# One decoder layer on one core: where the gate_r blocks, the squares of x and the embedding products stand, and how wide the attention products of the later keys are

## The chip, the cores and the metric

The kernel runs on one core of a Trainium2 chip. Its time is the device time of one execution, in microseconds (us). A core has TensorE (matrix products, which accumulate into PSUM), VectorE and ScalarE (elementwise work; ScalarE also evaluates functions and loads a table when the function's set changes), GpSimd, and SyncE, whose queue (SP) issues the DMAs. In the profile they are PE (with PEld for the loads of the stationary operand), ACT for ScalarE, DVE for VectorE, POOL for GpSimd, SP for SyncE. PSUM has eight banks of 128 x 512 floats here.

## The reference

One layer of a decoder for 256 tokens of width 2048, in float32.

```
h = rmsnorm(x, g_mix)
x_r, g_r, q, k, v, gate_r, gate_a = split(h @ w_in)       # 2816, 2816, then 5 of 2048
xc  = causal depthwise conv of width 4 (x_r)
r, i = sigmoid(block-diagonal products of xc + biases)     # 16 blocks of 176
a   = exp(-8 r softplus(-lambda));  u = sqrt(1 - a^2) * i * xc
s_t = a_t s_(t-1) + u_t                                    # scan over the tokens
y_r = (gelu(g_r) * s) @ w_rnn_out
q, k = rmsnorm per head (16 heads of 128)
z = q k^T / sqrt(128), only keys before the query
w = exp(log_sigmoid(z) + sum over later keys of log_sigmoid(-z))
y_a = (w @ v) @ w_attn_out
x = x + (sigmoid(gate_r) * y_r + sigmoid(gate_a) * y_a) @ w_o
x = x + (silu(g) * u) @ w_ffn_down,   g, u = split(rmsnorm(x, g_ffn) @ w_ffn_gu)   # 5632 each
x = x + sigmoid(rmsnorm(x, g_ple) @ w_ple_gate) * (p @ w_ple_proj)
```

## The kernel before

**Precision.** Every float32 operand is cut into a high part, rounded to the type that TensorE takes in one pass (`F32R`), and a low part, the rest. A product is three matmuls: high by high, high by low, low by high. `prod` (L534 to 538) does this with the activations as the stationary operand and 512 columns of weights moving, so its output is tokens x features; `mm3` (L447) the same for other operands; `dense` (L456) has a weight tile stationary and x moving, once with 512 columns (high and low part of x side by side, L466) and once with 256 (L470), so its output is features x tokens.

**Weights.** All weights lie packed in DRAM in the order in which they are used. `plan()` writes that order: one entry per block of products, cut into chunks of at most eight 128 x 128 tiles (512 KB; the first entry begins with two chunks of four tiles, `cuts_of`). `Stream` loads the chunks on the SP queue (`dma_to`, four buffers `w32`), up to 4 chunks ahead, and splits them up to 3 chunks ahead: ScalarE makes the high part (`whi`, L272), VectorE the low part (`wlo`, L273), four buffers each. `S_.after` hangs the load of another pair of rows of x (256 KB) behind a chunk. `Block` gives the split tiles of one entry to the code that uses them.

**Order of work.** The program is written in one order, and a planner in the build (the tile framework with its timeline) orders each engine's instructions by that order and by when it reckons that their operands are ready, and gives out buffers and PSUM banks. The engines then run their lists strictly in order.

**Stages.**

1. x comes transposed, 128 features x 256 tokens per row, in eight tiles `xt` of two rows. `next_xg` multiplies a tile by the gain and splits it (`xg`). `norm_sq` adds the squares of a tile to `acc0` (ScalarE squares, VectorE adds); `norm_end` sums over the partitions on TensorE (L519) and makes `rstd`, the scale of each token, along the free dimension; `norm_tokens` (L600) makes the same scales along the partitions, `rstd_tok`, with matmuls of two columns (L606).
2. The first product is a `dense` of four tiles: x_r for recurrence pairs 0 and 1 (L710). In its middle `norm_x` does all eight squares.
3. The recurrence, 11 pairs of 128 features (`for p in range(NPR)`, L714): `rnn_g` (projection g_r and gelu), for p up to 8 the projection and convolution of x_r for pair p + 2 (`rnn_conv`), and `rnn_gates` (the block-diagonal products, then sigmoid, exp, tanh, sqrt, the scan, and a split of the result). Behind pairs 1, 4, 6 and 9 (`GATE_R_AT`, L81) stands a gate_r block: `gate` and `block` (L689), 16 rows x 2 token halves x 3 matmuls of 512 columns, then a sigmoid.
4. The tail (`tail()`, L148) is a list of groups. `group` (L727) makes a 256 x 1024 output: both token halves by two column blocks, in four banks named 2, 4, 3, 8. Part of its rows go through a Strassen-like scheme with seven products in place of eight ("11", "T1", ... in the lists `SEVEN`, `SEVEN3`, `LONG`); it needs sums of weight tiles on VectorE (`Stream.summed`) and a fifth bank, B. `whole` (L775) joins the banks with the scheme's partial results. `pend` is a list of small tasks (transposes and splits for a later stage), one of which is done per weight row of a group.
5. Attention is laid over the q, k and gate_a blocks, two heads at a time (`step`, `ATT_AT`). Queries are 256 columns, keys two tiles of 128. `att_z` (L857) makes z with `mm3`, `att_e` the weights, `att_o` (L907) the products with v. For the second key tile (keys 128 to 255) the first 128 queries have no part: `att_z` computes them all the same, and `att_o` reads tiles `w1h`, `w1l`, in which those columns hold zeros (L391).
6. The last two groups (`pg`, L1071 on): `whole` gives the gate product, a sigmoid with the token scale, then for each column block and token half the embedding product (`p` by `w_ple_proj`, 6 matmuls), a multiplication, the addition of x1, and the store of 128 x 512 outputs (L1084). In the plan the two embedding chunks ("x", 0) and ("x", 1) stand at the end of the group.

Of the kernel before, what the change touches and what calls it, by code (L numbers as in the profile page):

```python
# [36 lines left out]
TWO = (0, 1)  # L37
NEG = -1e30
# [42 lines left out]
GATE_R_AT = {1: 0, 4: 1, 6: 2, 9: 3}  # L81


def plan():
# [6 lines left out]
    def proj(c0, p):  # L91
        dense("in", c0 + 2 * p, range(KD))
# [17 lines left out]
    dense("in", C_XR, range(KD), nt=4)  # L110
    for p in range(NPR):
        proj(C_GR, p)
        if p + 2 < NPR:
            proj(C_XR, p + 2)
        gates(p)
        if p in GATE_R_AT:
            block(C_GTR, GATE_R_AT[p])

    def tokens(name, g, w, cols, slots):


        for x in slots:
            if isinstance(x, int):
                t = [(w, x, m) for c in cols for m in c]
            elif x[0] == "x":
                t = [("pp", k, m) for k in range(2) for m in cols[x[1]]]
            elif isinstance(x, tuple):
                p = 2 * x[2]
                t = {1: [(p, 0), (p + 1, 0)], 2: [(p + 1, 1), (p, 1)]}.get(x[1], [])
                t = [(w, k, m) for k, c in t for m in cols[c]]  # L130
            elif x in ("T2", "T3", "T4"):
                t = []
            else:
                r, c = {"11": (0, 0), "21": (1, 0), "22": (1, 1), "T1": (0, 1)}[x]
                t = [(w, 2 * p + r, m) for p in TWO for m in cols[c]]
            out.append((("tok", name, g, x), t))

# [10 lines left out]
def tail():  # L148
# [11 lines left out]
    def dn(q):  # L160
# [8 lines left out]
            + wide("pg", "pg", [SEVEN + x] * 2))  # L169


TAIL = tail()
# [120 lines left out]
class Block:  # L293
# [7 lines left out]

    def chunk(self, c):
        a = self.cuts[c - 1] if c else 0
        return [(x, self[x]) for x in range(a, self.cuts[c])]
# [9 lines left out]
def tile_hybrid_block(ctx: ExitStack, tc: tile.TileContext, xT: bass.AP, x: bass.AP, pT: bass.AP,  # L314
# [53 lines left out]
    S_.dma_to(1)  # L368
    nc.sync.dma_start(t0[:, 256:], xT[:, 1, :])
    S_.after = {i: next_x for i in range(1, NPD)}  # L370
    S_.dma_to(2)
    nc.sync.dma_start(prm_sb, prm)
    S_.dma_to(4)
# [215 lines left out]
    for i in range(3):  # L589
        next_xg()  # L590
        S_.split_to(i + 2)

    def norm_x():
        with tc.issue_after(S_.hi_ins.ins):
            for i in range(NPD):
                norm_sq(xt[i], acc0, i == 0)

    rstd_tok = cst.tile([P, 4], F32, tag="rstdt", name="rstd_tok")

    def norm_tokens(acc, r):  # L600

        pn = psum()
        for t in range(2):
            for e in range(2):
                c = e * 256 + t * P
                nc.tensor.matmul(pn[:, 2 * t:2 * t + 2], acc[:, c:c + P], ones[:, :2],  # L606
                                 start=(e == 0), stop=(e == 1))
        rsqrt_mean(r, pn[:, :4], D)
# [92 lines left out]
    def rs_x(t):  # L701
        return rstd_tok[:, 2 * t:2 * t + 1]
# [7 lines left out]
    p01 = dense(in_keys(C_XR, 0), xg, 4, norm_x, next_xg)  # L710
    norm_end(acc0, rstd)
    rnn_conv(0, sums(p01[:2]))
    rnn_conv(1, sums(p01[2:]))
    for p in range(NPR):  # L714
# [3 lines left out]
        if p == 0:  # L718
            with tc.issue_after(S_.lo_ins.ins):
                decay_scales()  # L720
            norm_tokens(acc0, rstd_tok)
# [5 lines left out]
    def group(at, pairs, sums, after=None, also=()):  # L727

        name, g = at
        slots = [x for n, y, _, _, _, sl in TAIL if (n, y) == at for x in sl
                 if isinstance(x, int) or is_sum(x)]
        seq = [(n, q) for n, x in enumerate(slots) for q in products(x)]
        first, last = {}, {}
        for i, (_, (b, y, _, _)) in enumerate(seq):
            first.setdefault(b, i)  # L740
            last[b] = i
            if y in ("11", "T1", "T2", "T3"):
                last[y] = i
        plain8 = [i for i, (_, (b, y, _, _)) in enumerate(seq) if b == "8" and not isinstance(y, str)]
        assert "11" not in last or last["T1"] < plain8[0]
        banks, tile_ = {}, {}
        for i, (n, (b, y, p, c)) in enumerate(seq):
            if i == 0 or seq[i - 1][0] != n:
                if n in also:
                    also[n]()  # L750
                if n >= 3 and pend:
                    pend.pop(0)()
                w_ = S_.take(("tok", name, g, slots[n]))[0]
            if b not in banks:
                banks[b] = psum()
            ps = banks[b]
            if p is None:
                o = tok(pairs, *y)
            else:
                o = {"11": tok(pairs, 2 * p, 0), "21": tok(pairs, 2 * p + 1, 0), "22": sums[p][3],  # L760
                     "T1": sums[p][0], "T2": sums[p][1], "T3": sums[p][2],
                     "T4": tok(pairs, 2 * p + 1, 1)}[y]
            s = slice(c * 512, c * 512 + 512)
            prod(ps, o, w_[2][:, s], w_[3][:, s], i == first[b], i in (last[b], last.get(y)),
                 b in "B8")
            if y in ("11", "T1", "T2", "T3") and i == last[y]:
                t = tile_[y] = tl("T")
                actv(t, ps, AF.Copy)
                if y == "T2":
                    tt(tile_["T1"], tile_["T1"], t, ALU.subtract)  # L770
                if y == "T3" and after is not None:
                    after(tile_)
        return [banks[b] for b in "2438"], tile_

    def whole(at, pairs, sums, also=()):  # L775

        (q2, q4, q3, q8), t = group(at, pairs, sums, None, also)
        c11, c21, c12, c22 = t["11"], t["T3"], t["T1"], t["T2"]
        tt(c11, q2, c11, ALU.add)
        tt(c12, q3, c12, ALU.add)  # L780
        tt(c22, q8, c21, ALU.subtract)
        tt(c21, q4, c21, ALU.add)
# [74 lines left out]
    def att_z(hp):  # L857
        qt, kt_ = qs.pop(hp), ks.pop(hp)
        pss = []
        for kt in range(2):  # L860
            ps = psum()
            for e in range(2):
# [3 lines left out]
                mm3(o, (k_[:, c:c + P], k_[:, 256 + c:256 + c + P]), q_[:, :256], q_[:, 256:],  # L866
                    True, True)
# [39 lines left out]
    def att_o(hp):  # L907
        ws = zst.pop(hp)
        ps = psum()
        for e in range(2):  # L910
            o = ps[:, e * 256:e * 256 + 256]
            s = slice(e * 256, e * 256 + 256)
            for kt in range(2):
                v_ = vs[hp // 4 * 4 + hp // 2 % 2 * 2 + kt]
                c = hp % 2 * 256 + e * P
                mm3(o, (v_[:, c:c + P], v_[:, 512 + c:512 + c + P]), ws[kt][0][:, s],
# [153 lines left out]

    for g in range(2):  # L1071
        gate_ = whole(("pg", g), h3, sum3)
        for n, c in enumerate(gate_):
            actv(c, c, AF.Sigmoid, scale=rs2[:, n % 2:n % 2 + 1])
        for b in range(2):
            w_ = S_.take(("tok", "pg", g, ("x", b)))[0]
            for t in range(2):
                ps, c, x_ = psum(), gate_[2 * b + t], x1[t][2 * g + b]
                for k in range(2):
                    s = slice(k * 512, k * 512 + 512)  # L1080
                    prod(ps, tok(pts, k, t), w_[2][:, s], w_[3][:, s], k == 0, k == 1)
                tt(c, ps, c, ALU.mult)
                tt(c, c, x_, ALU.add)
                nc.sync.dma_start(out[t * P:t * P + P, (2 * g + b) * 512:(2 * g + b) * 512 + 512], c)  # L1084
# [62 lines left out]
```

## Time and profile before

| | |
|---|---|
| median of 3 runs | 1896.11 us (1894.04 to 1896.20) |
| the profiled execution | 1897.69 us, of which span 1896.0 us |
| mean granted TensorE clock | 0.998 |
| TensorE busy | 1881.1 us, 9006 matmuls |
| VectorE busy | 1379.6 us, 1646 instructions |
| ScalarE busy | 1160.1 us, 1532 instructions |
| read from HBM | 357.69 MB, 190 GB/s over the span |

The span runs from the first to the last instruction. Matmuls overlap: one of 512 columns is recorded with 391 ns, but the next starts some 227 ns after it, so the pace is read from the starts. A line such as `PE L466 MATMUL ps<-Q,whi 128x512 f32 x8` names engine, line of the kernel, output and inputs, the shape of the moving operand, and how many are merged; its first two numbers are start and length in us. What stands in brackets is the time that the engine was idle before it, and who ended that.

### The profile page before, as it was taken

How to read it: one execution, taken by the hardware profiler on the slowest of the kernel's cores; microseconds unless marked ns; L12 is line 12 of the kernel's file. 1: busy time of each engine (PE TensorE's matmuls, PEld its weight loads, DVE VectorE, ACT ScalarE, POOL GpSimd, SP SyncE). 2: the span in 40 equal slices, each digit the busy share in tenths (PEclk: the TensorE clock that was granted, in tenths of full speed). 3: DMA queues.
4: the chain of work that ended last, by engine and by line, in shares of the span. 5: the costliest groups of instructions: out<-in, count | busy, mean ns of one | idle time of the engine just before them, and what ended most of it. 6: DMA issues, size and time to landing. Idle time of an engine off the chain costs nothing.

```text
span 1896.0 us, 24012 instructions
## 1 busy us (share of the span) xinstructions
PE 1881.1 (99%) x9006; PEld 1581.3 (83%) x9006; DVE 1379.6 (73%) x1646; ACT 1160.1 (61%) x1532; POOL 2.2 (0%) x9
## 2 busy tenths in 40 slices
PE   8999999999999999999999999999999999999998
PEld 7988888888888888888888888888888888888887
DVE  7877676776687566665478988866886688855776
ACT  6878787874455566667445776644664456544663
POOL 0000000000000000000000000000000000000000
PEclk9999999999999999999999999999999999999999
DMA  6555555465635544545565555476356635565454
GB/s 239 176 197 178 204 175 194 168 227 191 247 134 193 194 157 156 178 152 171 194 228 200 205 190 215 173 251 218 134 186 242 235 123 208 180 211 191 166 193 150
DMA packets 101781, 361.36 MB, mean 191 GB/s; under 512 B 11424, under 2 KB 11808, under 8 KB 101664
## 3 DMA queue, kind: packets, MB, share of 16 engines
q1 hardware_dynamic: 101520, 359.82, 54.7%
q8 instruction: 70, 1.15, 0.2%
q14 instruction: 47, 0.39, 0.1%
q10 hardware_dynamic: 144, 0.01, 0.0%
HBM read 357.69 MB, written 2.10 MB: 190 GB/s over the span
## 4 chain that ended last, share of the span: by engine, by line
PE 93%; ACT 3%; DVE 2%; issue 1%; DMA 1%; SPq 0%; DVEq 0%; ACTq 0%
PE ps L537 26%; PE ps L538 26%; PE ps L536 26%; PE ps L466 7%; PE ps L470 4%; ACT H L347 1%; ACT L347 1%; PE ps L448 1%; PE ps L449 1%; PE ps L450 1%; DVE H L341 1%; DVE wlo L273 1%; ACT whi L272 1%; PE ps L1043 1%; DMA w<-in_w_dram 0%
## 5 line engine op out<-in xcount | busy, mean ns | idle before, releaser
L273 DVE TENSOR_TENSOR wlo<-w,whi 128x1024 fp32r<-128x1024 f32 (+3 forms) x580 | 701.1, 1215 | 361.3 <-ACT whi L272 357.4
L272 ACT ACTIVATE whi<-w 128x1024 fp32r<-128x1024 f32 (+3 forms) x580 | 606.3, 1052 | 465.6 <-PE ps L538 394.7
L537 PE MATMUL ps<-wlo,Q 128*128 128x512 f32 x2223 | 869.9, 391 | 3.1 <-DVE wlo L273 3.1
L538 PE MATMUL ps<-whi,Q 128*128 128x512 f32 x2223 | 868.1, 391 | 0.0
L536 PE MATMUL ps<-whi,Q 128*128 128x512 f32 x2223 | 796.5, 392 | 1.6 <-ACT whi L272 1.3
L537 PEld LDWEIGHTS ps<-wlo,Q 128*128 128x128 f32 x2223 | 418.4, 188 | 90.7 <-DVE wlo L273 6.0
L538 PEld LDWEIGHTS ps<-whi,Q 128*128 128x128 f32 x2223 | 418.4, 188 | 85.9
L536 PEld LDWEIGHTS ps<-whi,Q 128*128 128x128 f32 x2223 | 417.0, 188 | 87.4 <-ACT whi L272 2.0
L272 ACT ACTIVATE whi<-Q 128x1024 fp32r<-128x1024 f32 (+1 forms) x177 | 182.8, 1033 | 135.9 <-PE ps L538 117.5
L273 DVE TENSOR_TENSOR wlo<-Q,whi 128x1024 fp32r<-128x1024 f32 (+1 forms) x177 | 210.4, 1190 | 53.5 <-ACT whi L272 53.3
L466 PE MATMUL ps<-Q,whi 128*128 128x512 f32 x704 | 172.9, 395 | 1.1 <-ACT whi L272 1.1
L466 PEld LDWEIGHTS ps<-Q,whi 128*128 128x128 f32 x704 | 130.5, 191 | 26.6 <-ACT whi L272 1.9
L341 DVE TENSOR_TENSOR H<-ps,H 128x512 f32<-128x512 f32 (+1 forms) x168 | 99.0, 616 | 30.4 <-ACT H L347 16.2
L470 PEld LDWEIGHTS ps<-Q,wlo 128*128 128x128 f32 x704 | 91.1, 193 | 6.5 <-DVE wlo L273 2.9
L470 PE MATMUL ps<-Q,wlo 128*128 128x256 f32 x704 | 92.6, 284 | 2.5 <-DVE wlo L273 2.5
L256 DVE TENSOR_TENSOR Q<-Q,Q 128x1024 f32<-128x1024 f32 x76 | 92.8, 1221 | 0.8
L347 ACT ACTIVATE H<-ps 128x512 f32<-128x512 f32 (+1 forms) x122 | 60.2, 514 | 50.9 <-PE ps L466 31.1
L347 ACT ACT_TABLE_LOAD x66 | 84.7, 1283 | 2.7 <-DVE cT L574 1.5
L341 DVE TENSOR_TENSOR H<-H,H 128x512 f32<-128x512 f32 (+1 forms) x106 | 63.3, 604 | 1.8 <-ACT H L347 1.3
L347 ACT ACTIVATE Q<-H 128x512 fp32r<-128x512 f32 x41 | 25.2, 626 | 26.2 <-DVE H L341 25.7
L347 ACT ACTIVATE Q<-ps 128x512 fp32r<-128x512 f32 (+2 forms) x52 | 27.8, 565 | 19.7 <-DVE ps L341 8.8
L448 PE MATMUL ps<-Q,whi 128*128 128x256 f32 x140 | 39.7, 284 | 0.0
(131 smaller groups left out, 870.6 us busy)
## 6 DMA issues: line engine op xcount, KB each, us to landing
w<-in_w_dram SPq DMA_DIRECT2D x558, 512.0 KB, 3.8
Q<-in_w_dram SPq DMA_DIRECT2D x98, 512.0 KB, 6.7
w<-in_w_dram SPq DMA_DIRECT2D x16, 448.0 KB, 3.2
H<-in_x_dram SPq DMA_DIRECT2D x8, 256.0 KB, 5.9
out_dram<-H SPq DMA_DIRECT2D x8, 256.0 KB, 3.0
H<-in_xT_dram SPq DMA_DIRECT2D x7, 256.0 KB, 7.6
w<-in_w_dram SPq DMA_DIRECT2D x4, 320.0 KB, 5.1
w<-in_w_dram SPq DMA_DIRECT2D x2, 256.0 KB, 3.4
```

The costliest lines, as they stand in the source:

```text
L256: self.nc.vector.tensor_tensor(r[o], r[o], r[a], ALU.add)
L272: self.hi_ins = self.nc.scalar.activation(hi[:, :c], t[:, :c], AF.Copy)
L273: self.lo_ins = self.nc.vector.tensor_tensor(lo[:, :c], t[:, :c], hi[:, :c].bitcast(F32), ALU.subtract)
L341: nc.vector.tensor_tensor(o, a, b, op)
L347: nc.scalar.activation(o, i, f, **kw)
L448: nc.tensor.matmul(o, wt[0], xh, start=start, stop=False)
L449: nc.tensor.matmul(o, wt[0], xl, start=False, stop=False)
L466: nc.tensor.matmul(pss[e], wt[0], rhs(xs, k), start=(k == 0), stop=(k == n - 1))
L470: nc.tensor.matmul(pss[e][:, :256], wt[1], rhs(xs, k)[:, :256], start=False, stop=False)
L536: nc.tensor.matmul(ps, x[0], wh, start=start, stop=False, skip_group_check=goes_on)
L537: nc.tensor.matmul(ps, x[0], wl, start=False, stop=False, skip_group_check=goes_on)
L538: nc.tensor.matmul(ps, x[1], wh, start=False, stop=stop, skip_group_check=goes_on)
```

## The change

1. A new first group `("gtr", 0)` (list `HEAD`) computes gate_r blocks 0 and 1, all 16 rows of x plain, with `group`, which moves up in the file. The x_r products for pairs 0 and 1 follow as two ordinary projections. The other two gate_r blocks stand behind pairs 5 and 10.
2. In that group, the rows of x are scaled one tile per two chunks, and the squares of one tile are taken per chunk (slots 4 to 11). `x_scales` (slot 13) makes `rstd` as before and gets `rstd_tok` from it by two transposes; `norm_tokens` goes. A load of x hangs behind every second chunk; the second half of the first x tile and the parameters are loaded later in the queue.
3. The embedding chunks stand ahead of the last three rows of both last groups, and `embedded` makes their four products there. In the very last group (`LAST_GROUP`) the last three rows are not done row by row but bank by bank: all of 2, then 4, 3, 8. Each bank then gets its own run of join, sigmoid, multiplication, addition and store; the very last in two halves of 256 columns.
4. In `att_z` and `att_o` the matmuls of the second key tile have 128 query columns in place of 256.
5. `whole` joins in the order of the banks, with other tiles for two of the results.

```diff
-GATE_R_AT = {1: 0, 4: 1, 6: 2, 9: 3}
+GATE_R_AT = {5: 2, 10: 3}
...
-    dense("in", C_XR, range(KD), nt=4)
...
+    for stage, g, w, c0, c1, slots in HEAD:
+        tokens(stage, g, w, [list(range(c, c + 4)) for c in (c0, c1)], slots)
+    proj(C_XR, 0)
+    proj(C_XR, 1)
...
-            + wide("pg", "pg", [SEVEN + x] * 2))
+            + wide("pg", "pg", [SEVEN[:-3] + x + SEVEN[-3:]] * 2))
+HEAD = [("gtr", 0, "in", C_GTR, C_GTR + 4, list(range(KD)))]
...
     S_.dma_to(1)
+    S_.after = {2 * i: next_x for i in range(1, NPD)}
+    S_.dma_to(2)
     nc.sync.dma_start(t0[:, 256:], xT[:, 1, :])
-    S_.after = {i: next_x for i in range(1, NPD)}
-    S_.dma_to(2)
+    S_.dma_to(4)
     nc.sync.dma_start(prm_sb, prm)
-    S_.dma_to(4)
...
-    for i in range(3):
+    for i in range(2):
         next_xg()
         S_.split_to(i + 2)
...
+    def x_scales():
+        norm_end(acc0, rstd)
+        ps = psum()
         for t in range(2):
...
+            nc.tensor.transpose(ps[:, t * P:t * P + P], rstd[:, t * P:t * P + P], ident)
+            actv(rstd_tok[:, t:t + 1], ps[:, t * P:t * P + 1], AF.Copy)
...
+        if at == LAST_GROUP:
+            k = len(slots) - 3
+            rest = [q for q in seq if q[0] >= k]
+            seq = [q for q in seq if q[0] < k] + [q for b in "2438" for q in rest if q[1][0] == b]
...
-    p01 = dense(in_keys(C_XR, 0), xg, 4, norm_x, next_xg)
-    norm_end(acc0, rstd)
-    rnn_conv(0, sums(p01[:2]))
-    rnn_conv(1, sums(p01[2:]))
...
+    for i in range(2, NPD):
+        also.setdefault(2 * i - 3, []).append(next_xg)
+    for i in range(NPD):
+        also.setdefault(4 + i, []).append((lambda i: lambda: norm_sq(xt[i], acc0, i == 0))(i))
+    also[13] = [x_scales]
...
+    pss = group(("gtr", 0), xg, None, None, also)[0]
+    for b in range(2):
+        gtr.append([tl("C") for _ in range(2)])
+        for t in range(2):
+            actv(gtr[b][t], pss[2 * b + t], AF.Sigmoid, scale=rs_x(t))
+    for p in range(2):
+        rnn_conv(p, from_x(C_XR, p, "T", scale=False))
...
-                mm3(o, (k_[:, c:c + P], k_[:, 256 + c:256 + c + P]), q_[:, :256], q_[:, 256:],
-                    True, True)
+                mm3(o[:, c:], (k_[:, c:c + P], k_[:, 256 + c:256 + c + P]), q_[:, c:256],
+                    q_[:, 256 + c:], True, True)
...
-            s = slice(e * 256, e * 256 + 256)
...
-                mm3(o, (v_[:, c:c + P], v_[:, 512 + c:512 + c + P]), ws[kt][0][:, s],
+                a = kt * P
+                s = slice(e * 256 + a, e * 256 + 256)
+                mm3(o[:, a:], (v_[:, c:c + P], v_[:, 512 + c:512 + c + P]), ws[kt][0][:, s],
                     ws[kt][1][:, s], kt == 0, kt == 1)
...
     for g in range(2):
-        gate_ = whole(("pg", g), h3, sum3)
-        for n, c in enumerate(gate_):
-            actv(c, c, AF.Sigmoid, scale=rs2[:, n % 2:n % 2 + 1])
...
+        qs_, t_ = group(("pg", g), h3, sum3, also={len(SEVEN) - 3: embedded(g)})
+        for n, (q, c, op) in enumerate(zip(qs_, ("11", "T3", "T1", "T3"), (ALU.add,) * 3 + (ALU.subtract,))):
+            t, b = n % 2, 2 * g + n // 2
+            c, ps, o = t_[c], pp.pop(0), tl("T")
+            m = 512 if g == 0 or n < 3 else 256
+            for i in range(0, 512, m):
+                s = slice(i, i + m)
+                tt(o[:, s], q[:, s], c[:, s], op)
+                actv(o[:, s], o[:, s], AF.Sigmoid, scale=rs2[:, t:t + 1])
+                tt(o[:, s], ps[:, s], o[:, s], ALU.mult)
+                tt(o[:, s], o[:, s], x1[t][b][:, s], ALU.add)
+                nc.sync.dma_start(out[t * P:t * P + P, b * 512 + i:b * 512 + i + m], o[:, s])
```

## The prediction

> **What bounds the kernel now.** I read first the busy times by engine, then TensorE's waits, then windows around each place where TensorE stands idle, then single matmuls there, and last the end of the timeline.
>
> ```profile
> PE 1881.1 (99%) x9006; PEld 1581.3 (83%) x9006; DVE 1379.6 (73%) x1646; ACT 1160.1 (61%) x1532; POOL 2.2 (0%) x9
> ...
> PE ps L537 <- DVE wlo L273: 3.1, 5, 1.1
> PE ps L470 <- DVE wlo L273: 2.5, 2, 1.9
> ...
> 5.50:10.00 4.50, 4.01 (x17) 3.11 (x16) 2.81 (x8) 2.42 (x7) 0.41 (x1) 1.00 0.95 313
> 10.00:20.00 10.00, 8.71 (x48) 7.53 (x49) 8.92 (x15) 9.24 (x17) 0.00 (x0) 1.00 1.03 406
> 20.00:28.00 8.00, 6.14 (x37) 5.29 (x36) 7.48 (x11) 8.00 (x13) 0.00 (x0) 1.00 0.37 136
> 28.00:32.00 4.00, 4.00 (x15) 3.38 (x15) 3.54 (x4) 0.34 (x1) 0.00 (x0) 0.57 0.71 249
> ...
> 100.00:110.00 10.00, 8.94 (x37) 6.42 (x36) 8.56 (x13) 6.95 (x9) 0.00 (x0) 1.00 0.36 129
> 370.00:380.00 10.00, 8.99 (x39) 6.78 (x38) 6.49 (x9) 7.33 (x11) 0.00 (x0) 1.00 0.35 132
> 400.00:410.00 10.00, 8.43 (x40) 6.54 (x39) 6.92 (x8) 9.93 (x17) 0.00 (x0) 1.00 0.14 55
> 410.00:414.00 4.00, 4.00 (x12) 3.11 (x12) 2.84 (x3) 3.97 (x5) 0.00 (x0) 0.57 0.37 133
> 1840.00:1850.00 10.00, 8.95 (x39) 7.08 (x39) 10.00 (x13) 6.83 (x8) 0.00 (x0) 1.00 0.18 33
> ```
>
> TensorE is busy 99% of the span, so only two things can move the time: fewer or shorter matmuls, and the few places where TensorE stops. In the windows (length, then busy time of TensorE, its weight loads, VectorE, ScalarE, GpSimd, granted clock, DMA share) these are the first 32 us, the gate_r block behind recurrence step 1 (100 us), the one behind step 9 (370), the start of the recurrence's output product (400) and the border between the last two groups (1840). Everywhere else ten microseconds are full. TensorE waits there for a weight chunk's low half: ScalarE and VectorE split every chunk (1.06 and 1.22 us) and are late. In two windows the granted clock drops to 0.57: an idle stretch also costs half clock for a while, 4 us × 0.43 = 1.7 us each.
>
> ```profile
> 8.41 1.10 PE L466 MATMUL ps<-Q,whi 128*128 128x512 f32 x4
> 10.65 2.11 PE L466 MATMUL ps<-Q,whi 128*128 128x512 f32 x8 [1.14 <-ACT whi L272]
> 24.62 1.11 PE L470 MATMUL ps<-Q,wlo 128*128 128x256 f32 x8
> 27.59 1.58 PE L470 MATMUL ps<-Q,wlo 128*128 128x256 f32 x8 [1.86 <-DVE wlo L273]
> 32.21 0.86 PE ps L519 x4
> 58.00 0.95 PE L606 MATMUL ps<-ones,acc 128*128 128x2 f32 x8
> 770.51 1.04 PE L836 MATMUL ps<-ident,H 128*128 128x128 f32 x8
> 1890.59 0.39 PE L538 MATMUL ps<-whi,Q 128*128 128x512 f32 x1
> 1891.74 0.69 DVE L341 TENSOR_TENSOR H<-H,H 128x512 f32<-128x512 f32 x1
> ```
>
> From start to start a 512-column matmul takes 0.227 us in long runs, a 256-column one 0.120 (the 24 attention ones from 776.84 to 779.71). Loss is what start-to-start exceeds these.
>
> **The change, part by part.** The sum is made against the profiled execution, 1897.69 us (span 1896.0 and 1.69 around it); the median of the runs, 1896.11, is 1.58 lower.
>
> *Start.* Losses now: from 8.41, four matmuls need 0.91 and the next start at 10.65: 1.3; likewise 0.8 at 14.35; from 24.62, eight need 0.96 and the next wait until 27.59: 2.0; half clock 1.7. Together 5.8. The cause: a 512 KB chunk carries two rows of x, so DMA brings 768 KB per chunk (406 GB/s, share 1.03), four scalings of x stand beside each split, and all eight squares come in one lump at 20.3 to 28 on ScalarE (0.62 each) and VectorE (adds of 0.69), ahead of a split.
> The new first group does 12 matmuls of 512 columns per chunk, 2.72 us (before: 8 × 0.227 + 8 × 0.120 = 2.77), but one row of x: DMA 640 KB, 235 GB/s; ScalarE 1.06 + 0.50 + 0.62 = 2.2; VectorE 1.22 + 0.48 + 0.69 = 2.4. All fit in 2.72. The squares have no lump. The second chunk's 512 KB stand 1.28 MB down the SP queue; now ScalarE's waits for DMA end at 7.8 (1.02 MB down the queue) and at 9.5 (1.65 MB), so about 8.5, split high at 9.6, while the first row's 12 matmuls (five at 0.43, as now until 7.7) end at 9.3. Loss left about 0.8; gain **5.0**. Each SP issue (0.43) is as before; x's second half goes one place back, the parameters three: they land near 11 instead of 8.27, and one small VectorE operation (the query gain) waits for them and could hold a split back 1.3. Bounds: a gain of 2.0 (one lump with its half clock stays) to 5.8. The matmuls are the same number: 128 of the four-tile product plus two blocks of 96 go, the group's 192 and two two-tile products of 64 come. No GpSimd work moves.
> *Token scales.* The eight passes of L606 (58.00 to 58.81, 0.81) go, two transposes come (0.79 / 8 each, 0.2): **-0.6**. The scale's Ln, Exp, two copies and four sigmoids lie beside 22 us of matmuls for x_r pairs 0 and 1; without that cover they cost about 5.
> *Blocks.* The first block's loss (start to start 0.8 + 0.6 + 0.15 between 100.7 and 108.2) came from the recurrence step's elementwise work standing in ScalarE's queue before splits. Steps 1 and 4 now have no block behind them; steps 2 and 3 had none, with no loss. **-1.5** (0 to -2).
> Around steps 9 and 10 I count the loss now as 0.9 + 0.4 + 0.2 (370 to 381), 1.4 + 0.5 (407 to 410), 1.7 half clock: 5.1. Steps 9 and 10 have only one projection, 16.2 us of matmuls (341.14 to 357.33 between their gates), against ScalarE work of 6 splits (6.1), evacuation and gelu (1.3), the gate and split passes (4.7) and four table loads of 1.28: about 17. Now a block of 22 us stands between; afterwards they adjoin, and the block follows both, ahead of the output product. One stall moves earlier, one grows, the one at the product's start goes: **0**, bounds -3 and +5.
> *Attention.* Of the 256-column matmuls 12 per head pair, 96 in all, get 128 columns. Nothing in the trace shows such a product. Lower end: in proportion to columns, 0.120 - 0.0535 = 0.066, -5.1. Upper end: at the pace of the plain fp32 product (L519: two products of 256 columns in four passes, 0.86, so 0.215 for 128 columns), 96 × 0.0955 = +9.2. The nearest rows, the 128-column transposes (0.099) and the two-column products (0.101), agree on a floor under one matmul with its weight load; I take 0.10: **-1.9**. TensorE waits for nothing in that stage, so it counts in full. The Trainium skill ("TensorE: Matmul & The Clock Gate", section "LDWEIGHTS (loading the stationary operand)") gives 128 columns of weights 107 ns; as an estimate that makes -1.2, and both rows here lie just below it.
> *Last groups.* The 24 matmuls of the embedding (5.4 us) used to stand between the gate product of group 0 and group 1, while VectorE was full (10.00 of 10) with evacuation and weight sums. They move ahead of the last three weight rows; their two splits (2.4 of VectorE) go too, 3.0 us of cover is lost. Group 1's first three chunks are split ahead, so I take a third: **+1.0** (0 to +3, with half clock).
> At the end, now: last matmul starts 1890.59, one product and one sum until 1892.43, DMA to 1896.0. Then: subtract, sigmoid, multiply, add of 256 columns (0.42 + 0.50 + 0.42 + 0.42), the second half's last two (0.8), and 0.3 to 0.6 of VectorE still at the third quarter, whose four operations take 2.8 while a quarter's nine matmuls take 2.04. About 2.9 against 1.4; one more output DMA issue of 0.34 hides behind this. **+1.5** (+0.8 to +3).
> *No cost:* the new roles of tiles in `whole` (the same four operations), `columns`.
> Sum: -5.0 - 0.6 - 1.5 + 0 - 1.9 + 1.0 + 1.5 = -6.5: 1891.2 on the profiled execution's scale, 1889.6 on the median's.
>
> **Rivals.** (B) The other side: 128-column products run at the plain fp32 pace. For it: the old code pads the later keys' weights with zeros to 256 columns where leaving them out was easier. Against it: a product records one pass, the fp32 one two. Then +11.1: 1900.7, slower. It cancels the other parts' 4.6 from 0.168 us per matmul (96 × 0.048) and makes the kernel slower by over 0.2% from 0.207.
> (C) ScalarE falls further behind at steps 9 and 10: 3 us more stall and one more half clock, 1.7: 1894.3. For it: ScalarE busy 9.5 of 10 at 360 to 370. Against: before, the second stall was as large with a block between. The same page of the Trainium skill ("HAM oscillation — how this bites in real kernels") wants an idle gap over about 3.4 us for a lower clock; by that it would be 1892.6. The trace has half clock after a loss of 2.0, so I keep 1.7.
> (E) The start does not do what it says: splits wait behind squares or parameters and the 5.0 stays: 1894.6. For it: VectorE at 2.4 of 2.72.
> (D) Matmul time in proportion to columns: 3.2 more, 1886.4. Against: no row below 0.099.
>
> **Numbers.** Forecast 0.46, B 0.25, C 0.14, E 0.09, D 0.06. Within 0.2% (about what a measurement tells from no change) is 1892.3 to 1899.9. Faster: forecast 0.40, D 0.06, C and E 0.07, B 0.01: 0.54. Slower: B 0.15, the rest 0.05: 0.20; same 0.26. The forecast's own terms give 1885 to 1894; with B the range is 1885 to 1902.
>
> **What would show it.** No wait of TensorE over 1 us between 10 and 45 us and no half clock there (start); none behind step 1; the stalls at 373 and 407 replaced by one or two before 400; TensorE's start-to-start in the 128-column products, 0.10 or 0.21, and one record each or two; last matmul to span end 6.9 instead of 5.4. I am wrong if those products take over 0.17, or if a new wait over 2 us appears at steps 9 and 10 or between the last groups.

## The result and the profile after

The changed kernel takes 1900.76 us (median of ten runs, 1899.50 to 1902.94), the kernel before 1895.88 in the runs beside it: ratio 1.0029, interval 1.0019 to 1.0038, so slower by 0.3%. The forecast was 1889.6, faster; the time lies inside the range, at its far end. The profiled execution of after took 1902.26 us with a span of 1900.5, 4.5 more than the 1896.0 of before.

In the changed kernel the lines have moved: `prod` is L546 to 548, `mm3` L458 to 460, the splits are L277 (high part) and L278 (low part), the loads L227, and ScalarE's and VectorE's other operations go through helpers at L357 and L351.

In what follows, the loss of a stretch is what TensorE's starts exceed the pace of 0.2266 us after a 512-column matmul, 0.1195 after one of 256 columns and 0.100 after a narrower one, added up.

| loss of TensorE, us | before | after |
|---|---|---|
| 0 to 45 us, the first products | 9.5 | 6.2 |
| 45 to 130, recurrence steps 0 to 1 | 2.4 | 0.5 |
| 130 to 350 | 1.0 | 1.2 |
| 350 to 425, steps 9 and 10 and the start of the output product | 6.0 | 15.1 |
| 425 to 1780 | 4.8 | 5.6 |
| 1780 to 1830 | 0.5 | 0.6 |
| 1830 to 1860, border of the last two groups | 1.4 | 0.6 |
| start of the last matmul to the end of the span | 5.4 | 8.4 |

Two rows turned bad by 9.1 and 3.0 us, three turned good by 0.8 to 3.3, and the other three rose by less than 1. First the engines' busy times, from the page of after:

```profile
PE 1879.0 (99%) x9000; PEld 1576.3 (83%) x9000; DVE 1377.5 (72%) x1649; ACT 1157.5 (61%) x1532; POOL 2.2 (0%) x9
```

TensorE is busy 2.1 us less and the span is 4.5 longer: the time lies in waits. TensorE's waits in after (line that waits, what it waits for, us in total, times, longest):

```profile
PE ps L546 <- ACT whi L277: 6.8, 7, 1.8
PE ps L547 <- DVE wlo L278: 3.7, 6, 1.0
```

Before, TensorE waited mostly for low parts, which VectorE makes. Now the largest sum is for high parts, which ScalarE makes. The windows of after say where (length, then busy time of TensorE, its weight loads, VectorE, ScalarE, GpSimd, granted clock, DMA share, GB/s):

```profile
10.00:20.00 10.00, 9.94 (x44) 7.83 (x44) 10.00 (x18) 9.81 (x21) 0.00 (x0) 1.00 1.04 402
20.00:28.00 8.00, 6.54 (x28) 4.81 (x27) 8.00 (x13) 7.02 (x11) 0.00 (x0) 1.00 0.44 148
28.00:32.00 4.00, 4.00 (x19) 3.28 (x18) 2.24 (x3) 1.84 (x3) 0.00 (x0) 1.00 0.86 261
100.00:110.00 10.00, 10.00 (x64) 9.02 (x63) 9.41 (x20) 8.72 (x14) 0.00 (x0) 1.00 0.48 165
...
360.00:370.00 10.00, 10.00 (x62) 8.80 (x60) 4.12 (x6) 9.91 (x15) 0.00 (x0) 1.00 0.48 148
370.00:380.00 10.00, 7.71 (x38) 5.72 (x37) 8.34 (x13) 6.40 (x10) 0.00 (x0) 1.00 0.42 132
380.00:390.00 10.00, 7.94 (x33) 5.69 (x32) 4.19 (x5) 9.91 (x14) 0.00 (x0) 1.00 0.42 139
...
400.00:410.00 10.00, 5.71 (x19) 3.37 (x20) 7.29 (x7) 7.31 (x9) 0.00 (x0) 1.00 0.45 183
410.00:414.00 4.00, 3.70 (x11) 2.66 (x11) 3.59 (x4) 3.56 (x5) 0.00 (x0) 0.72 0.35 123
```

At 28 us the granted clock is 1.00 instead of 0.57 and at 100 us TensorE is full: these parts worked. From 370 to 410 it is nearly full (9.81 of 10) only between 390 and 400, with ScalarE at 9.91 of 10 just before (360 to 370) and in the middle (380 to 390). Single matmuls of after, at a wait of the start, at the longest wait, in attention and at the end (start, length, in brackets the idle time and who ended it):

```profile
20.65 0.39 PE L548 MATMUL ps<-whi,Q 128*128 128x512 f32 x1
21.84 1.20 PE L546 MATMUL ps<-whi,Q 128*128 128x512 f32 x4 [0.79 <-ACT whi L277]
...
407.57 0.39 PE L548 MATMUL ps<-whi,Q 128*128 128x512 f32 x1
409.81 0.96 PE L546 MATMUL ps<-whi,Q 128*128 128x512 f32 x3 [1.85 <-ACT whi L277]
...
780.16 0.22 PE L458 MATMUL ps<-w1h,Q 128*128 128x128 f32 x1
780.23 0.28 PE L459 MATMUL ps<-w1l,Q 128*128 128x128 f32 x1
780.34 0.27 PE L460 MATMUL ps<-w1h,Q 128*128 128x128 f32 x1
780.45 0.33 PE L458 MATMUL ps<-H,Q 128*128 128x256 f32 x1
...
1892.16 0.39 PE L548 MATMUL ps<-whi,Q 128*128 128x512 f32 x1
```

The 128-column products start 0.07, 0.11 and 0.11 us after one another, with one record each, so they are nowhere near the plain float32 pace. And ScalarE's list in after, at those two waits:

```profile
14.49 1.06 ACT L277 ACTIVATE whi<-w 128x1024 fp32r<-128x1024 f32 x1 [0.18 <-DMA w<-in_w_dram]
15.46 0.89 ACT L357 ACTIVATE Q<-H,gm_sb 128x256 fp32r<-128x256 f32 x2
16.25 0.62 ACT L357 ACTIVATE H<-H 128x512 f32<-128x512 f32 x1
...
20.74 1.04 ACT L277 ACTIVATE whi<-w 128x1024 fp32r<-128x1024 f32 x1
...
399.11 1.06 ACT L277 ACTIVATE whi<-Q 128x1024 fp32r<-128x1024 f32 x1 [2.74 <-DMA Q<-in_w_dram]
402.80 2.00 ACT L277 ACTIVATE whi<-Q 128x1024 fp32r<-128x1024 f32 x2 [2.63 <-DVE Q L261]
404.82 1.28 ACT L357 ACT_TABLE_LOAD   x1
406.12 1.27 ACT L357 ACTIVATE H<-ps,rstd_tok 128x512 f32<-128x512 f32 x2
407.40 1.28 ACT L791 ACT_TABLE_LOAD   x1
408.70 1.06 ACT L277 ACTIVATE whi<-w 128x1024 fp32r<-128x1024 f32 x1
```

Between the splits at 14.49 and 20.74 ScalarE does eight scalings and four squares of x and no split: the squares, written one per chunk, stand in a lump again. From 404.82 on, the two sigmoids of the fourth gate_r block, between two table loads, stand ahead of the split that TensorE waits for. Before that, ScalarE itself waited 2.74 us for a DMA. SP's list (start and length of a run of loads, from 355 us on) shows when that load went out:

```profile
356.71 37.44 SPq L227 DMA_DIRECT2D w<-in_w_dram  x12
394.20 2.01 SPq L227 DMA_DIRECT2D Q<-in_w_dram  x4
```

The Q tiles are the weights that the output product sums for its seven-product scheme. They are issued at 394.20, behind twelve chunk loads that need buffers which late splits have not freed; the product wants them at 399. (In before they go out at 378.06, but there the list has another order, with seven chunk loads ahead of them from 355 on; an experiment below has the same twelve.) At the end, VectorE's list of after has no pause from 1890.54 on:

```profile
1888.96 1.29 DVE L351 TENSOR_TENSOR H<-ps,H 128x512 f32<-128x512 f32 x2 [4.93 <-PE ps L548]
1890.54 1.89 DVE L351 TENSOR_TENSOR H<-ps,H 128x512 f32<-128x512 f32 x3 [0.30 <-PE ps L548]
...
1896.08 0.74 DVE L351 TENSOR_TENSOR H<-H,H 128x256 f32<-128x256 f32 x2
```

It idles 4.93 us until 1888.96 and then runs until 1896.8: the banks, meant to end in four stages, end close together.

### The profile page after: what moved, and what is told of

Its sections match the earlier page's. It is cut to its first block, busy times and chain, and to the rows that moved or that the text cites. A ratio compares the mean times of both kernels' runs of the same rounds, so it can differ in the third digit from the quotient of the medians.

```text
span 1900.5 us, 24015 instructions
## 1 busy us (share of the span) xinstructions
PE 1879.0 (99%) x9000; PEld 1576.3 (83%) x9000; DVE 1377.5 (72%) x1649; ACT 1157.5 (61%) x1532; POOL 2.2 (0%) x9
## 4 chain that ended last, share of the span: by engine, by line
PE 95%; ACT 2%; DVE 1%; DMA 1%; issue 1%; SPq 0%; DVEq 0%; ACTq 0%
PE ps L547 26%; PE ps L548 26%; PE ps L546 26%; PE ps L476 8%; PE ps L480 4%; PE ps L459 1%; PE ps L460 1%; PE ps L458 1%; ACT L357 1%; ACT H L357 1%; ACT whi L277 1%; DMA w<-in_w_dram 1%; PE ps L1062 1%; DVE wlo L278 0%; DVE H L351 0%
## 5 line engine op out<-in xcount | busy, mean ns | idle before, releaser
L278 DVE TENSOR_TENSOR wlo<-w,whi 128x1024 fp32r<-128x1024 f32 (+2 forms) x580 | 700.3, 1214 | 378.9 <-ACT whi L277 374.7
L277 ACT ACTIVATE whi<-w 128x1024 fp32r<-128x1024 f32 (+2 forms) x580 | 606.9, 1052 | 471.9 <-PE ps L548 412.9
L546 PE MATMUL ps<-whi,Q 128*128 128x512 f32 x2223 | 793.9, 392 | 7.1 <-ACT whi L277 6.8
L546 PEld LDWEIGHTS ps<-whi,Q 128*128 128x128 f32 x2223 | 417.1, 188 | 95.9 <-ACT whi L277 11.0
L277 ACT ACTIVATE whi<-Q 128x1024 fp32r<-128x1024 f32 (+1 forms) x177 | 182.6, 1032 | 138.2 <-PE ps L548 115.2
L278 DVE TENSOR_TENSOR wlo<-Q,whi 128x1024 fp32r<-128x1024 f32 (+1 forms) x177 | 209.7, 1187 | 54.2 <-ACT whi L277 53.9
L351 DVE TENSOR_TENSOR H<-ps,H 128x512 f32<-128x512 f32 (+1 forms) x170 | 98.1, 608 | 28.9 <-PE ps L548 16.1
L357 ACT ACTIVATE H<-ps 128x512 f32<-128x512 f32 (+1 forms) x122 | 60.3, 515 | 53.0 <-PE ps L548 28.4
L480 PE MATMUL ps<-Q,wlo 128*128 128x256 f32 x704 | 91.3, 283 | 0.0
L351 DVE TENSOR_TENSOR H<-H,H 128x512 f32<-128x512 f32 (+2 forms) x107 | 63.1, 597 | 3.1 <-ACT H L357 2.6
L357 ACT ACTIVATE Q<-H 128x512 fp32r<-128x512 f32 x41 | 25.1, 624 | 27.1 <-DVE H L351 26.5
L460 PE MATMUL ps<-Q,wlo 128*128 128x256 f32 x140 | 39.7, 284 | 1.1 <-DVE wlo L278 1.1
L458 PE MATMUL ps<-Q,whi 128*128 128x256 f32 x140 | 39.7, 283 | 0.0
```

Source lines behind the costliest of these rows:

```text
L277: self.hi_ins = self.nc.scalar.activation(hi[:, :c], t[:, :c], AF.Copy)
L278: self.lo_ins = self.nc.vector.tensor_tensor(lo[:, :c], t[:, :c], hi[:, :c].bitcast(F32), ALU.subtract)
L351: nc.vector.tensor_tensor(o, a, b, op)
L357: nc.scalar.activation(o, i, f, **kw)
L458: nc.tensor.matmul(o, wt[0], xh, start=start, stop=False)
L460: nc.tensor.matmul(o, wt[1], xh, start=False, stop=stop)
```

## The experiments

The theory after the result: the 9 us at 350 to 425 come from the place of the fourth gate_r block, because ScalarE is the slower engine in steps 9 and 10 and nothing now stands between them; the start loses by squares ahead of splits; the end by the bank-by-bank form.

**The place of the fourth block.** In the changed kernel it goes back behind step 9:

```diff
-GATE_R_AT = {5: 2, 10: 3}
+GATE_R_AT = {5: 2, 9: 3}
```

> The changed kernel with the last gate_r block back behind step 9 (the third stays behind step 5). Theory (steps 9 and 10 side by side overload ScalarE, the splits come late, and with them the loads): the loss of TensorE between 360 and 420 us falls from 15.1 us to about the 5.9 that the kernel before lost there, and the time from 1900.8 to about 1891.6. Rival (the block's place right ahead of the output product is at fault, not the two steps): the same 1891.6. If the place of the block does not matter at all: 1900.8.

Measured: 1891.52 against 1895.61 of before, ratio 0.9979 (0.9970 to 0.9988). The loss from 350 to 425 falls from 15.1 to 4.3 us. The windows of this kernel:

```profile
360.00:370.00 10.00, 9.24 (x41) 7.36 (x40) 4.05 (x5) 9.91 (x14) 0.00 (x0) 1.00 0.34 107
370.00:380.00 10.00, 9.70 (x42) 7.38 (x41) 9.06 (x11) 4.87 (x6) 0.00 (x0) 1.00 0.84 313
```

ScalarE falls behind in step 9 (9.91 of 10) and has caught up by the next window (4.87) beside the block, whose chunks then come at 313 GB/s. One number of the change is what made it slower. Both readings had given this time; the runs that follow tell them apart. The same move alone, in the kernel before:

```diff
-GATE_R_AT = {1: 0, 4: 1, 6: 2, 9: 3}
+GATE_R_AT = {1: 0, 4: 1, 6: 2, 10: 3}
```

> The kernel before with one thing changed: the fourth gate_r block stands behind step 10 in place of step 9. Theory (with nothing between steps 9 and 10 and the block behind both, ScalarE's lateness costs the new kernel its 9 us): TensorE's loss between 360 and 430 us rises from 6.0 to about 15 us, time 1895.6 + 9 = 1904.6. Rival (it takes the new kernel's other moves, the blocks taken away from steps 1, 4 and 6, too): 1895.6 to 1898.

Measured: 1904.74 against 1895.43, ratio 1.0049 (1.0036 to 1.0063); the loss from 350 to 425 is 14.8 instead of 6.0. So the move costs 9.3 us with and without the rest of the change.

**Is it ScalarE's time, or only that the block adjoins the product?** In the changed kernel the functions of steps 9 and 10 are left out: gelu, sigmoid, exp, tanh and sqrt become plain copies with the same scales, which need no tables. The passes, the matmuls and the order stay. This kernel does not compute these functions for the last two steps.

```diff
-        actv(g, g, AF.Gelu_apprx_tanh)
+        actv(g, g, AF.Gelu_apprx_tanh if p < 9 else AF.Identity)
...
-        actv(r, r, AF.Sqrt)
+        actv(r, r, AF.Sqrt if p < 9 else AF.Identity)
```

> The changed kernel, where the recurrence steps 9 and 10 leave their functions out: gelu, sigmoid, exp, tanh and sqrt become plain scaled copies of the same size, so ScalarE loads no function tables for them (eight loads of 1.28 us, 10 us less). All else is as in the changed kernel. Theory (ScalarE's time in these two steps is the root, the late loads and the stall at the output product follow from it): the loss between 360 and 420 us falls from 15.1 us to below 4, time about 1889.5. Rival (the block ahead of the output product has its own cost): the stalls from 399 to 411 us, about 7.8 with the half clock, stay, and only those before go: about 1894.

Measured: 1888.78, ratio 0.9963 (0.9951 to 0.9976); the loss from 350 to 425 is 2.0. The windows:

```profile
370.00:380.00 10.00, 10.00 (x50) 8.46 (x49) 8.06 (x10) 8.22 (x15) 0.00 (x0) 1.00 0.61 210
380.00:390.00 10.00, 10.00 (x45) 8.28 (x45) 6.73 (x9) 3.16 (x4) 0.00 (x0) 1.00 0.88 327
```

TensorE is full where it lost 2.3 and 2.1, though the block still stands behind step 10, and SP issues the Q loads 12.1 us earlier, behind the same twelve chunk loads:

```profile
382.07 2.09 SPq L227 DMA_DIRECT2D Q<-in_w_dram  x4
```

So the root is ScalarE's time in two adjoining steps, the ten table loads that are missing here (55 in place of 65 at that line, 1.28 us each) above all: ScalarE's busy time falls by 13.4 us, and these are 12.8 of it. The late DMAs did not stay when it went. That a late split holds a chunk buffer, and the buffer holds SP's list, is read from the trace and was not tried by itself.

**Behind step 8.** Another place for that block in the changed kernel:

```diff
-GATE_R_AT = {5: 2, 10: 3}
+GATE_R_AT = {5: 2, 8: 3}
```

> The changed kernel with the last gate_r block behind step 8: steps 9 and 10 still stand side by side, but no block stands between step 10 and the output product. Theory (two short steps side by side): most of the 15.1 us of loss stays, 1898 to 1901. Rival (the block ahead of the output product): the loss falls to about 6, 1891.6.

Measured: 1898.40, ratio 1.0016 (1.0007 to 1.0024). The time is what the theory gave, but not its way there. Steps 9 and 10 have no large stall; the whole lateness falls due at once, at the start of the output product. TensorE there:

```profile
394.17 0.39 PE L548 MATMUL ps<-whi,Q 128*128 128x512 f32 x1
402.86 0.80 PE L546 MATMUL ps<-whi,Q 128*128 128x512 f32 x1 [8.30 <-ACT whi L277]
```

and ScalarE, meanwhile:

```profile
393.43 1.28 ACT L357 ACT_TABLE_LOAD   x1
...
399.66 1.28 ACT L357 ACT_TABLE_LOAD   x1
...
401.77 1.99 ACT L277 ACTIVATE whi<-Q 128x1024 fp32r<-128x1024 f32 x2
```

Four table loads and the passes of the last step, from 393.43 to 401.77, stand ahead of the product's first split. Step 10's elementwise work needs matmuls beside it as well, and here none are left: the block already stood ahead of step 9.

**Both remaining blocks there.** With the old end of the last groups (the experiment on the end, below), the third block goes behind step 8 and the fourth behind step 9:

```diff
-GATE_R_AT = {5: 2, 9: 3}
+GATE_R_AT = {8: 2, 9: 3}
```

> As the changed kernel with the old end, the third gate_r block behind step 8 and the last behind step 9. Theory (a block behind a short step gives ScalarE 22 us of matmuls with few splits' worth of other work, so the stalls behind step 9, 0.95 + 0.4, go; those at the output product, 1.4 + 0.5, stay): loss between 350 and 425 us from 4.3 to about 2.9, time 1887.5. Rival (without the block behind step 5 nine steps in a row let the lateness build up): a new stall before step 8, 1889 to 1892.

Measured: 1886.83, ratio 0.9953 (0.9939 to 0.9967). The loss from 350 to 425 is 2.3, against 4.3 with the block behind step 9 alone.

**The end.** The changed kernel with the last groups as they were in before (embedding chunks at the end, `whole`, no bank by bank):

```diff
-            + wide("pg", "pg", [SEVEN[:-3] + x + SEVEN[-3:]] * 2))
+            + wide("pg", "pg", [SEVEN + x] * 2))
...
-        if at == LAST_GROUP:
+        if False:
...
```

> The changed kernel with the old end: embedding chunks last in both groups, whole, no order by banks. Theory (three banks of the last group end almost together, so VectorE has most of its last operations left when TensorE is done): from the last matmul's start to the end of the span 5.4 us as before in place of 8.3, at the border of the last two groups 0.7 more loss: time 1900.8 - 2.9 + 0.7 = 1898.6. Rival (the longer end comes from the output DMAs, one more issue and slower landing): the end stays near 8, 1900.8 to 1901.5.

Measured: 1898.43, ratio 1.0013 (1.0004 to 1.0022), 2.3 less than after. From the start of the last matmul to the end of the span it takes 5.45 us instead of 8.38. This and the block's place undone, by the edits shown:

> The changed kernel with the last block behind step 9 and the old end of the last two groups; the new start and the narrower attention products stay. Theory (the parts add up: 1891.5 with the block moved back, and the old end took 2.4 off the changed kernel): 1889.1. Rival (the end's gain depends on the rest): 1890.5 to 1891.5.

Measured: 1888.94, ratio 0.9969 (0.9958 to 0.9981). The two gains add.

Why the new end takes 8.4 and not the 6.9 forecast: in the trace of after, the four banks of the last group end 16, 14, 9 and 0 matmuls before the end, where bank by bank means 27, 18, 9 and 0. The planner mixed banks 2, 4 and 3. Here TensorE is held to the written order, with the block behind step 9:

```diff
...
+            if at == LAST_GROUP and n >= len(slots) - 3 and b != seq[i - 1][1][0]:
+                with tc.issue_after(done.ins):
+                    done = prod(*args)
...
```

> The changed kernel with the last block behind step 9 and, in the last group, TensorE held to the written order: bank 2 whole, then 4, 3, 8 (in the changed kernel the planner mixed the first three banks, so that they end almost together). Theory (that mixing piles VectorE's work at the end): from the last matmul's start to the end of the span about 6.9 us in place of 8.4, time 1891.5 - 1.4 = 1890.1. Rival (VectorE's sixteen operations and the DMA take that long in any order): 8.4, 1891.5.

Measured: 1891.01, ratio 0.9976 (0.9968 to 0.9985), 0.5 under the same kernel with mixed banks, which the times don't tell apart; the tail does, in the trace: from the start of the last matmul to the end of the span 7.33 instead of 8.38. VectorE at the end of this one:

```profile
1881.40 1.69 DVE L351 TENSOR_TENSOR H<-ps,H 128x256 f32<-128x256 f32 x4 [0.67 <-PE ps L548]
...
1884.39 0.43 DVE L351 TENSOR_TENSOR H<-H,H 128x256 f32<-128x256 f32 x1
```

It now pauses before the last bank, as the forecast had it, and ends 3.84 us after the last matmul's start (1880.98), 3.45 after its end; the forecast had reckoned 2.9. The order of the banks was 1.0 of the 1.5 us of error. Even in the written order this end is 1.9 longer than the old one.

**The start.** With the block behind step 9 and the old end, each tile's squares are held behind the split issued last, so that the planner can't pull them ahead:

```diff
-        also.setdefault(4 + i, []).append((lambda i: lambda: norm_sq(xt[i], acc0, i == 0))(i))
+        def held(i):
+            with tc.issue_after(S_.hi_ins.ins):
+                norm_sq(xt[i], acc0, i == 0)
+        also.setdefault(4 + i, []).append((lambda i: lambda: held(i))(i))
```

> As the changed kernel with the last block behind step 9 and the old end (1888.9), and the squares of x in the first group held on ScalarE behind the split issued last at their place in the program (in the changed kernel the planner pulls them ahead of splits, to 6 to 23 us). Theory (the first group's stalls at 20.7 and 22.6 us, 0.96 + 0.83, come from scalings and squares standing in ScalarE's queue between 15.5 and 20.7 us before a split): the loss of the first 45 us falls from 6.3 to about 4.8, time 1887.4. Rival (the scalings of x alone keep ScalarE there, or the loads are late): 1888.9.

Measured: 1886.45, ratio 0.9951 (0.9939 to 0.9964), 2.5 less than without the hold. The loss from 0 to 45 falls from 6.3 to 3.9. The windows:

```profile
10.00:20.00 10.00, 9.94 (x44) 7.89 (x43) 8.99 (x18) 8.86 (x18) 0.00 (x0) 1.00 1.02 399
20.00:28.00 8.00, 8.00 (x37) 6.63 (x36) 7.51 (x8) 5.77 (x8) 0.00 (x0) 1.00 0.74 230
```

From 20 to 28 TensorE is full. From 10 to 20 VectorE and ScalarE are busy 8.99 and 8.86 of 10; without the hold it is 10.00 and 9.94. The opposite, with the same two parts undone, has all squares written at one slot:

```diff
-        also.setdefault(4 + i, []).append((lambda i: lambda: norm_sq(xt[i], acc0, i == 0))(i))
+        also.setdefault(8, []).append((lambda i: lambda: norm_sq(xt[i], acc0, i == 0))(i))
```

> As the changed kernel with the last block behind step 9 and the old end, but all eight squares of x written at one place (slot 8) in place of one per chunk. Theory (the planner orders them by when x has landed, so where they are written hardly counts): 1888.9, loss of the first 45 us within 0.5 of 6.3. Rival (one lump of squares delays the splits as in the kernel before): 2.0 to 3.7 more, 1891 to 1892.6.

Measured: 1889.76, ratio 0.9970 (0.9958 to 0.9981), 0.8 more than 1888.94 and not told apart from it by time. Its trace misses the theory's bound: it has a gap of 2.44 us at 20.7 and half clock behind it, and 8.3 of loss in place of 6.3. Some 1.7 of these 2.0 are the half clock, which does not come in every execution (last section). So how much the written place of the squares counts, as long as the planner may move them, stays open between nothing and the 0.8 of the times; that holding them counts is clear.

**The 128 columns.** The kernel before with only this part of the change:

```diff
-                mm3(o, (k_[:, c:c + P], k_[:, 256 + c:256 + c + P]), q_[:, :256], q_[:, 256:],
-                    True, True)
+                mm3(o[:, c:], (k_[:, c:c + P], k_[:, 256 + c:256 + c + P]), q_[:, c:256],
+                    q_[:, 256 + c:], True, True)
```

> The kernel before with the 128 query columns for the second key tile alone. Theory (one pass, about 0.098 us per such matmul by the new kernel's trace, which counts in full): 24 matmuls per head pair take 1.4 to 1.5 us less over all eight pairs, 1895.6 - 1.5 = 1894.1. Rival (plain fp32 pace): 1904.8.

Measured: 1895.33, ratio 1.0000 (0.9992 to 1.0009). A gain of 1 us is too small for these times; a loss of 9 is excluded. In the trace, the stretch from the first of these products to the last is 0.97 shorter.

**Together.** Both blocks behind steps 8 and 9, the squares held, the old end:

> The changed kernel with the old end, the squares held behind the splits, and the last two gate_r blocks behind steps 8 and 9. Theory (the gains of the runs before add up, -2.5 for the squares and -2.1 for the blocks on 1888.9): 1884.3. Rival (they share what they save, since both remove lateness of ScalarE): 1885.5 to 1886.5.

Measured: 1884.43 (1883.92 to 1886.58) against 1895.37, ratio 0.9946 (0.9932 to 0.9960): faster than both kernels, by 0.5% and 0.9%. The median is the theory's sum; but two of the five runs (1886.14 and 1886.58) lie where the rival put them, so that the gains add in full is likely and not certain. TensorE's largest waits that are left:

```profile
PE ps L588 <- DVE ones_r L398: 1.5, 1, 1.5
PE ps L546 <- ACT whi L277: 1.5, 2, 1.3
```

The first is the warm-up before any weights. With two more, of 0.4 and 0.3, they make 3.7 us.

## Why the prediction was wrong

The forecast lost by one term, the steps 9 and 10. That the time still lies inside the range is luck: the range reaches to 1902 for rival B, the slow products, and the forecast's own terms end at 1894. By terms, on the profiled executions:

| term, us | forecast | measured |
|---|---|---|
| start | -5.0 (-5.8 to -2.0) | -3.3 |
| token scales | -0.6 | -0.6 (eight passes against two transposes, 0.100 each) |
| block behind step 1 | -1.5 | -1.9 |
| steps 9 and 10 | 0 (-3 to +5) | +9.1 |
| attention | -1.9 (-5.1 to +9.2) | -1.0 |
| border of the last groups | +1.0 (0 to +3) | -0.8 |
| end | +1.5 (+0.8 to +3) | +3.0 |
| sum | -6.5 | +4.5 (spans: +4.5) |

**Steps 9 and 10: the step that failed.** "One stall moves earlier, one grows, the one at the product's start goes: 0" compared 16.2 us of matmuls with about 17 of ScalarE, step by step. Two things in it were wrong. One is an input: the 17 counts four table loads to a step. The traces of both kernels show five in step 9, because gelu runs between the two sigmoid passes; and step 10 has five in after (377.17 to 389.28), where it had three in before (402.80, 405.02, 411.56) with the sigmoid table still loaded from the block's own sigmoid (387.69). So the move itself gives ScalarE two loads more, 2.6 us, by the counts of the kernel with the block behind step 9 and of after:

```profile
L357 ACT ACT_TABLE_LOAD x63 | 80.8, 1283 | 1.1
L357 ACT ACT_TABLE_LOAD x65 | 83.4, 1283 | 1.2
```

(In the kernel before, the same move makes 68 out of 66.) The other is the way of counting: it treated a shortage as paid within its step. The runs show that it is handed on: ScalarE's work of step 9 runs into step 10, that of step 10 into the product, and the late loads and the block's own sigmoids then add to it. The stall at the product's start, which was to go because the block now covers it, became the largest. Rival C named this mechanism and priced it at 4.7 more; it was 9.1. Its counterargument, that "the second stall was as large with a block between", was the misreading: the stalls on both sides of the block in before were what remained after the block had let ScalarE catch up. The prediction's own sign of being wrong, a new wait over 2 us at these steps, did not appear: from 350 to 425 the longest is 1.85 us, and the 9.1 are a sum of many.

**The start** did not do what the change says, in part (rival E's condition). The working put one square per chunk beside one split, 2.2 us of ScalarE in 2.72. The written order isn't the order that runs: the planner brings squares and scalings forward as soon as x has landed. In before they were held by an order written into the code, in after they are free. Of the gain of 3.3, some 1.4 is the half clock at 28 us, which the change need not have removed: with the 128 columns alone the start is that of before, and its execution lost 8.1 there without any half clock. The signs that the prediction gave for the start, no wait over 1 us after 10 us and no half clock, came true all the same. Held squares give 2.4 more.

**The end** was under-sized: the direction and most of the size came from the right chain, but the term took the banks in their written order. With that order held, the tail is 7.3 and not the 6.9 reckoned; as planned it is 8.4.

**Attention.** Rival B falls, although the time of after is almost the 1900.7 that it gave: agreement of a total shows nothing about its cause. The 128-column products start 0.098 us apart on average, just under the 0.10 that the floor gave, and all 192 products of z and of v, 96 of them narrowed, take 1.4 us less together. It would be 2.0, but the 96 that kept 256 columns rise from 0.1195 to 0.126 on average, and the stage as a whole gains 1.0. The estimate from the Trainium skill ("TensorE: Matmul & The Clock Gate", section "LDWEIGHTS (loading the stationary operand)"), -1.2, came nearer as a sum, though its 107 ns of weight load per product is above the 98 ns measured from start to start. Rival D, time in proportion to columns, falls too.

**Border.** The cover that was to be lost cost nothing: the loss fell from 1.4 to 0.6. VectorE is as full as before (9.89 of 10 from 1840 to 1850). With the old end in the changed kernel the loss is 1.0, so only 0.4 of the 0.8 belongs to the moved embedding; why it helped, perhaps by the two splits that moved with it, was not tried, and where the rest comes from is open.

**Half clock.** The forecast priced a stall of some 2 us with 1.7 of half clock behind it, against the rule of the Trainium skill ("TensorE: Matmul & The Clock Gate", section "HAM oscillation — how this bites in real kernels"), which wants an idle gap over about 3.4 us. Here half clock followed waits well below that, though not all of them, as the last section shows.

## What to carry to other kernels

Where an in-order engine prepares operands for TensorE, add up its work and its lateness over all adjoining stages, not per stage. Here the place of one block of matmuls, between two short stages or behind them, was worth 9.3 us. Count the table loads in the trace too: they depend on what the planner puts side by side. Read in the trace the order that runs before pricing work that is "spread" in the source; if the place matters, hold it there. When a total fits a rival, look for that rival's own sign before believing it.

## What was not expected of the hardware

**A gap of 2.0 us sometimes brings half clock and sometimes doesn't.** In before, the wait of 1.86 us ahead of 27.59 has half clock behind it (eight matmuls take 1.58). With the 128 columns alone, nothing at that place is changed, and its timeline reads:

```profile
24.68 1.11 PE L470 MATMUL ps<-Q,wlo 128*128 128x256 f32 x8
27.67 1.22 PE L470 MATMUL ps<-Q,wlo 128*128 128x256 f32 x8 [1.87 <-DVE wlo L273]
```

The same wait, and full clock. Two shorter gaps, 1.08 and 0.76 us, had half clock behind them in the changed kernel with the old end, and 1.5 and 0.7 had none in the one with both blocks moved. In the wait of 8.3 us of the kernel with the block behind step 8, half clock began some 3 us after the last matmul's start and lasted 10 us, until 5 us after the wait had ended. The figure of the Trainium skill ("TensorE: Matmul & The Clock Gate", section "HAM oscillation — how this bites in real kernels"), 3.4 us, fits that last case; as a bound under which nothing happens it does not fit the gaps of 2.0 and less.

The clock in the traces goes further. Inside the kernel, half clock lasts 3.41 us each time (10.24, three times as long, in that last case). Within an execution its beginnings lie whole multiples of 3.413 us apart: in before 28.23, 410.52 and, behind the last matmul, 1895.32, which are 112 and then 435 multiples apart. So cut each execution into pieces of 3.41 us along this grid. Here are the piece of before that ends where half clock begins, the next one, and the two pieces of the 128 columns alone in which the same wait falls:

```profile
24.82:28.23 3.41, 1.55 (x13) 1.34 (x12) 3.21 (x5) 3.41 (x4) 0.00 (x0) 1.00 0.01 2
28.23:31.64 3.41, 3.41 (x12) 2.83 (x12) 3.31 (x3) 0.12 (x1) 0.00 (x0) 0.50 0.74 261
...
23.31:26.72 3.41, 2.49 (x15) 2.03 (x13) 3.01 (x5) 3.41 (x6) 0.00 (x0) 1.00 0.35 131
26.72:30.14 3.42, 2.47 (x15) 2.22 (x16) 3.42 (x4) 1.72 (x2) 0.00 (x0) 1.00 0.43 146
```

In before the whole wait, 1.86 us, lies in one piece; in the other kernel the grid cuts it into 0.93 and 0.94. The fourteen traces agree: from 8 us to the last matmul, every piece in which TensorE idles 1.51 us or more has half clock in the piece behind it, and none with 1.48 or less has. By this, where the grid falls decides about a gap near 2 us. It is read from the traces; no run was made to test it, and two pieces that reach beyond the last matmul, with 1.79 and 1.90 idle, had full clock behind them.

**Products of 128 moving columns** in the float32 type of one pass start 0.098 us apart, hardly below the 0.120 of 256 columns, and with a median of 0.061 for the first of three and 0.111 for the others. To halve the columns saves a sixth, and part of that is lost in the products beside them.

**Table loads in line with splits.** Each takes 1.28 us in ScalarE's list, and ten fewer of them in two steps of 16 us of matmuls made the kernel 12.0 us shorter (1888.78 against 1900.76), though ScalarE is busy only 61% of the span. That is close to their whole 12.8 us; a stretch of half clock, 1.7 us, went with them.
